# Two decoder layers on one core: five raw weight buffers instead of four, two half-tiles fewer, and one constant loaded later

## The chip, the cores and the metric

The kernel runs on one core of a Trainium2 chip. The time is the device time of one execution in microseconds (us), and the median of several runs is what counts. Besides the plain runs there is one profiled execution, from which the profile and the trace come. TensorE is called PE in them, its weight loads PEld, VectorE DVE, ScalarE ACT, GpSimd POOL and SyncE SP. SP only issues DMAs here.

## The reference

Two layers, each with three residual sub-layers on x of 512 tokens by 1024 features, all float32:

```
x += 1/2 * post(SwiGLU_1(pre(x)))          # 1024 -> 2 x 2816 -> 1024
h = pre(x);  P = h @ W_in                  # one projection for both branches
A = HGRN2 gated recurrence (4 heads)       # -> W_bA
B = sliding-window attention with sinks    # -> W_bB
x += post((sigmoid(gA)*A + sigmoid(gB)*B) @ W_out)
x += 1/2 * post(SwiGLU_2(pre(x)))

def swiglu(h, w_gate, w_up, w_down):
    return (jax.nn.silu(h @ w_gate) * (h @ w_up)) @ w_down
```

pre and post are RMS norms with gains of their own. The two SwiGLU networks of each layer, four in all, hold most of the arithmetic.

## The kernel before

**Products.** Every matrix product is done in three matmuls on operands split in two: a high part, which is the value cast to PE's reduced 32-bit type (fp32r), and a low part, the value minus its high part. `mm3` issues high x high, high x low, low x high. So each operand, weight or activation, needs a cast (on ACT) and a subtraction (on DVE) before PE can use it. For activations this is the function `split(src)`: line 400 casts on ACT, line 401 subtracts on DVE. For the weights it is the class `Stream` (object `ws`): `load` brings a raw unit of 128 x 1024 numbers from DRAM to a buffer "w" (lines 241 and 244, DMAs on SP's queue); `split` makes a pair `whi`, `wlo` out of it (cast at L324 on ACT; L331 subtracts on DVE, or, for some kinds of units, L328 and an accumulating DMA on POOL's queue, L329). There are `W32` raw buffers and `WS` = 6 pairs of `whi` and `wlo`. `ahead` splits as long as pairs are free: the pair of a unit comes free with the last matmul that reads it.

**An FFN.** After the first blocks, the function `fast` runs over blocks j of 128 hidden features. `sevenths` makes a block of gate and up with seven products in place of eight (a Strassen-like scheme, with sums of weights made in `split`, and sums of activations held in half-tiles); its copy of the first product is at L864 on ACT, its combinations on DVE are at L874, L876, L881 and L882. Then come Silu (L894, ACT) and the product with it (DVE), and the block z joins the list a. In the last block, `early` is called after the second of the seven products: it splits the first four blocks of a (`EARLY` = 4, with L400 and L401), so that the down product can begin at once:

```
def early():
    if j == FT - 1:
        for i in range(EARLY):
            a[i] = split(a[i])
```

The down product follows, in quarters and with seven products again. Its weights are quarter units: the function `quarter` sums raw units where needed (L267, L268, L276, L277, DVE), casts in two halves (L281, ACT, two casts a unit) and subtracts in two halves (L286, DVE). The raw units of a quarter come in four pieces, one DMA each. The sums need further quarters of the weight too, which `load` brings as a "side load" into eight half-tiles (L252, each in two pieces of 256 columns), issued right behind the load of a unit u that stands in `self.side`.

**Pools.** The half-tiles are all of one pool, tag "s", made by `big()`: 128 x 512 numbers, 2 KB a partition, `SLOTS` of them. The blocks of a, their splits, x's operands and their splits, the copies and sums of `sevenths` and of the down product and the side loads all take their slots there. A slot is given out in the order of the calls, and the new owner waits for the last reader of the old one.

**Order.** Only PE's order is written by hand: the tile framework is told that PE is scheduled manually, and an `Order` object interleaves generators by due times. The order on ACT, DVE and on the queues of SP and POOL is decided when the kernel is built, by the framework's scheduler, which sees when slots of the pools come free. SP's queue runs in order.

**Start.** The tiles of x (`xs[k]`, eight of them) are loaded in turn with the first `W32` raw units (`ws.load(k + 1)` where k < W32). Then the constants: `ident`, `half_ident` (the identity folded to 128 x 64, used in the mixer at L1015 to L1017), `dist`, `mask`, `lb_in`, `hgh` and `sink`.

Of the kernel before, what the change touches and what calls it, by code (L numbers as in the profile page):

```python
# [15 lines left out]
P = 128  # L16
# [10 lines left out]
EPS = 1e-6  # L27
LEVELS = (1, 2, 4, 8, 16, 32, 64)
MASKS = [(m, n) for b in LEVELS[:-1:2] for m, n in ((b, b), (2 * b, 2 * b), (2 * b, b))] + [(64, 64)]
SLOTS = 61  # L30

WAIT = dict(
    first=0.0, spread=2300.0, squares=1700.0, lay=34500.0, laid=770.0, normed=7600.0, final=2600.0,
    head=2600.0, level=1720.0, chunks=1270.0, blocks=350.0, norm=2370.0, gate=8000.0,
    values=1200.0, scores=2000.0, exp=9000.0, shares=4500.0, turn=1900.0, turned=3000.0, rest=1200.0, lent=3500.0, apart=4000.0, block=2000.0, pair=4000.0, att0=1260.0, att1=12300.0,
)
W32, WS, AHEAD, TAIL, PLAIN, FIRST, EARLY, LATE = 4, 6, 3, 4, 4, 7, 4, 8
TURN = 0
LEAD = 8
ORDER = ("p1", "p6", "p2", "p7", "p5", "p4", "p3")  # L40
# [5 lines left out]
def trunk(ctx: ExitStack, tc: tile.TileContext, xin, wall, gains, lbT, hgain, sinks, c_dist, c_mask, c_ident, out):  # L46
    nc = tc.nc
# [11 lines left out]
    def nm(s):  # L59
        seq[0] += 1  # L60
        return f"{s}_{seq[0]}"

    def big(dt=F32, shape=None):
        return sb.tile(shape or [P, S], dt, tag="s", name=nm("s"), bufs=SLOTS)

# [9 lines left out]
    def const(shape, name, dt=F32):  # L75
        return cp.tile(shape, dt, tag=name, name=name)
# [1216 lines left out]
            ws.load(k + 1)  # L1293
    ident = const([P, P], "ident")
    nc.sync.dma_start(ident, c_ident)
    half_ident = const([P, 64], "half_ident")
    nc.sync.dma_start(half_ident[:64], c_ident[:64, :64])
    nc.sync.dma_start(half_ident[64:], c_ident[64:, 64:])
    dist = const([P, 256], "dist")
    nc.sync.dma_start(dist, c_dist)  # L1300
    mask = const([P, len(MASKS) - 1, 32], "mask", I32)
# [5 lines left out]
    nc.sync.dma_start(hgh, hgain.partition_broadcast(P))  # L1307
    sink = const([P, DEPTH, NH], "sink")
    nc.sync.dma_start(sink, sinks.partition_broadcast(P))
    for k in range(KT):  # L1310
        pre.add(k)
        if k in (0, 2, 4):
            ws.split()
        if k > 2:
            pre.square(k - 3)
# [127 lines left out]
```

## Time and profile before

| what | before |
|---|---|
| median of 3 runs | 2112.13 us (2110.0 to 2112.33) |
| profiled execution | 2114.98 us |
| its span | 2113.2 us |
| mean granted clock of TensorE | 0.998 |

The span is the time from the first to the last instruction that the trace shows; the execution is somewhat longer. In the rows of a timeline stand the start and the duration in us, the engine, the line of the kernel, the operation and the tiles (`out<-in`), then partitions x elements; `x2` at the end means two such instructions in a row, shown in one line, and a bracket gives the idle time of the engine ahead of it with what ended it. In a row of waits stand the total time, how many times, and the longest. A row of groups gives the number of instructions, their busy time and the mean ns of one, then the idle time ahead of them and what ended it. A matmul's duration overlaps with the next one's: what counts is the distance between starts, 0.24 us for 512 columns at full clock.

### The profile page before, as it was taken

Reading aid. Unit: us, or ns where it says so; the run is one execution under the profiler, and the core shown is the slowest. Engines: PE = TensorE matmul, PEld = TensorE weight load, DVE = VectorE, ACT = ScalarE, POOL = GpSimd, SP = SyncE. Lnnn points to the kernel's source line nnn. Section 1 sums busy time; section 2 is a strip of 40 time slices with the busy share of each in tenths; the row PEclk is TensorE's granted clock in tenths of the full one; section 3 lists DMA queues with packets and bytes.
Section 4 is the critical chain, followed back from the end, with each engine's and each line's share of the span. In section 5 each row is a group of like instructions: output and inputs, shape, how many; then the busy total and the mean of one; then the engine's idle time right before and its main releaser. Section 6 shows DMA issues by size and latency. Waiting matters only on the chain.

```text
span 2113.2 us, 35244 instructions
## 1 busy us (share of the span) xinstructions
PE 2101.1 (99%) x13549; PEld 1875.3 (89%) x13549; DVE 1551.0 (73%) x2705; ACT 1124.9 (53%) x1900; POOL 154.6 (7%) x188
## 2 busy tenths in 40 slices
PE   9999999999999999999999999999999999999998
PEld 7899988887888999998899998888778989999987
DVE  5777886767676777779587778767686767777884
ACT  6555554446445555556355556454554545555562
POOL 0111000000000011110001110000000000111000
PEclk9999999999999999999999999999999999999999
DMA  7577754321237357774437775632122553677651
GB/s 234 150 181 181 188 146 137 106 70 61 70 100 209 120 125 175 180 194 125 160 109 175 181 185 150 189 116 95 51 71 70 135 185 110 154 182 181 183 165 45
DMA packets 148072, 298.36 MB, mean 141 GB/s; under 512 B 16992, under 2 KB 74816, under 8 KB 147904
## 3 DMA queue, kind: packets, MB, share of 16 engines
q1 hardware_dynamic: 122416, 228.16, 32.8%
q0 software_dynamic: 25344, 67.91, 18.5%
q8 instruction: 106, 1.74, 0.3%
q14 instruction: 62, 0.51, 0.1%
q10 hardware_dynamic: 144, 0.05, 0.0%
HBM read 213.43 MB, written 14.73 MB: 108 GB/s over the span
## 4 chain that ended last, share of the span: by engine, by line
PE 81%; DVE 9%; ACT 5%; issue 2%; DMA 2%; SPq 1%; ACTq 0%; DVEq 0%
PE acc L115 60%; PE aux L115 19%; ACT whi L324 2%; DMA w<-wall 2%; PE aux L125 1%; DVE s L401 1%; DVE wlo L331 1%; DVE wlo L286 1%; PE acc L125 1%; ACT s L400 1%; ACT m L894 1%; ACT wlo L328 1%; SPq L241 1%; DVE tt L268 0%; DVE w L267 0%
## 5 line engine op out<-in xcount | busy, mean ns | idle before, releaser
L115 PE MATMUL acc<-s,whi 128*128 128x256 f32 (+1 forms) x4968 | 1069.9, 312 | 1.7 <-ACT whi L324 0.9
L115 PEld LDWEIGHTS acc<-s,whi 128*128 128x128 f32 x4968 | 809.9, 191 | 54.5 <-issue 2.1
L115 PE MATMUL acc<-s,wlo 128*128 128x256 f32 (+1 forms) x2484 | 770.5, 310 | 0.1
L115 PEld LDWEIGHTS acc<-s,wlo 128*128 128x128 f32 x2484 | 474.5, 191 | 25.9 <-DVE wlo L331 0.4
L324 ACT CAST whi<-w 128x1024 fp32r<-128x1024 f32 (+1 forms) x341 | 317.4, 949 | 252.2 <-PE aux L115 103.4
L115 PE MATMUL acc<-whi,s 128*128 128x512 f32 x1264 | 413.6, 393 | 0.0
L324 ACT CAST whi<-tt 128x1024 fp32r<-128x1024 f32 x154 | 161.7, 1050 | 341.4 <-DVE tt L318 188.9
L331 DVE TENSOR_TENSOR wlo<-w,whi 128x1024 fp32r<-128x1024 f32 (+1 forms) x181 | 218.5, 1216 | 134.8 <-ACT whi L324 128.4
L115 PEld LDWEIGHTS acc<-whi,s 128*128 128x128 f32 x1264 | 237.0, 188 | 55.7 <-issue 3.2
L331 DVE TENSOR_TENSOR wlo<-tt,whi 128x1024 fp32r<-128x1024 f32 x154 | 188.2, 1222 | 102.5 <-ACT whi L324 102.5
L115 PE MATMUL acc<-wlo,s 128*128 128x512 f32 x632 | 246.8, 391 | 1.0 <-DVE wlo L286 1.0
L329 POOL DMA_DIRECT2D wlo<-w x160 | 138.2, 865 | 1266.3 <-ACT wlo L328 856.7
L115 PE MATMUL aux<-s,whi 128*128 128x256 f32 x1232 | 225.1, 283 | 0.0
L115 PE MATMUL aux<-whi,s 128*128 128x512 f32 x592 | 196.8, 390 | 0.0
L115 PEld LDWEIGHTS aux<-s,whi 128*128 128x128 f32 x1232 | 192.2, 192 | 0.0
L115 PE MATMUL aux<-s,wlo 128*128 128x256 f32 x616 | 174.4, 283 | 0.1
L115 PEld LDWEIGHTS acc<-wlo,s 128*128 128x128 f32 x632 | 118.7, 188 | 25.8 <-DVE wlo L286 2.4
L115 PEld LDWEIGHTS aux<-whi,s 128*128 128x128 f32 x592 | 111.1, 188 | 22.9
L328 ACT ACTIVATE wlo<-w 128x1024 fp32r<-128x1024 f32 (+1 forms) x160 | 129.9, 845 | 0.0
L400 ACT CAST s<-s 128x512 fp32r<-128x512 f32 (+1 forms) x164 | 88.6, 581 | 65.9 <-DVE s L459 60.6
L115 PEld LDWEIGHTS aux<-s,wlo 128*128 128x128 f32 x616 | 118.3, 192 | 0.3 <-DMA wlo<-w 0.3
L115 PE MATMUL aux<-wlo,s 128*128 128x512 f32 x296 | 115.2, 389 | 0.0
(185 smaller groups left out, 2136.6 us busy)
## 6 DMA issues: line engine op xcount, KB each, us to landing
w<-wall SPq DMA_DIRECT2D x267, 512.0 KB, 3.7
wlo<-w POOLq DMA_DIRECT2D x83, 512.0 KB, 5.5
w<-wall SPq DMA_DIRECT2D x288, 128.0 KB, 3.1
wlo<-w POOLq DMA_DIRECT2D x77, 256.0 KB, 3.3
x_d<-s SPq DMA_DIRECT2D x48, 256.0 KB, 2.1
s<-x_d SPq DMA_DIRECT2D x48, 256.0 KB, 5.5
w<-wall SPq DMA_DIRECT2D x34, 256.0 KB, 2.9
s<-wall SPq DMA_DIRECT2D x64, 128.0 KB, 3.5
```

Source lines behind the costliest of these rows:

```text
L115: nc.tensor.matmul(o, lhsT, rhs, start=start, stop=stop)
L125: nc.tensor.transpose(o, src, ident)
L241: nc.sync.dma_start(w.rearrange("p (m c) -> p m c", m=4) if c is None else w[:, c], a)
L286: nc.vector.tensor_tensor(it.lo[:, h[c]], w[c], it.hi[:, h[c]].bitcast(F32), op=ALU.subtract)
L324: i = nc.scalar.copy(it.hi[:, c], w[:, c])
L328: nc.scalar.mul(it.lo[:, c], w[:, c], -1.0)
L329: nc.gpsimd.dma_start(it.lo[:, c].bitcast(F32), w[:, c], accum_op=ALU.add)
L331: nc.vector.tensor_tensor(it.lo[:, c], w[:, c], it.hi[:, c].bitcast(F32), op=ALU.subtract)
L400: nc.scalar.copy(hi, src)
L401: nc.vector.tensor_tensor(lo, src, hi.bitcast(F32), op=ALU.subtract)
L894: nc.scalar.activation(out=m[:, 0:2, :], in_=m[:, 0:2, :], func=AF.Silu)
```

## The change

One raw weight buffer more (`W32`, 4 to 5, each of 4 KB a partition), two half-tiles fewer (`SLOTS`, 61 to 59, each of 2 KB a partition), and the two DMAs of `half_ident` issued after the other constants. At the start `W32` also sets how many raw units are loaded in turn with x's tiles, and in `Stream.split` and `quarter` how far the loads run ahead (`self.load(self.freed + W32)`).

```diff
-SLOTS = 61
+SLOTS = 59
...
-W32, WS, AHEAD, TAIL, PLAIN, FIRST, EARLY, LATE = 4, 6, 3, 4, 4, 7, 4, 8
+W32, WS, AHEAD, TAIL, PLAIN, FIRST, EARLY, LATE = 5, 6, 3, 4, 4, 7, 4, 8
...
     ident = const([P, P], "ident")
     nc.sync.dma_start(ident, c_ident)
-    half_ident = const([P, 64], "half_ident")
-    nc.sync.dma_start(half_ident[:64], c_ident[:64, :64])
-    nc.sync.dma_start(half_ident[64:], c_ident[64:, 64:])
     dist = const([P, 256], "dist")
...
     sink = const([P, DEPTH, NH], "sink")
     nc.sync.dma_start(sink, sinks.partition_broadcast(P))
+    half_ident = const([P, 64], "half_ident")
+    nc.sync.dma_start(half_ident[:64], c_ident[:64, :64])
+    nc.sync.dma_start(half_ident[64:], c_ident[64:, 64:])
     for k in range(KT):
         pre.add(k)
```

## The prediction

> **What bounds the kernel now.** I read the busy times first, then the shares of the chain that ended last, then what PE waited for.
>
> ```profile
> span 2113.2 us, 35244 instructions
> PE 2101.1 (99%) x13549; PEld 1875.3 (89%) x13549; DVE 1551.0 (73%) x2705; ACT 1124.9 (53%) x1900; POOL 154.6 (7%) x188
> PE 81%; DVE 9%; ACT 5%; issue 2%; DMA 2%; SPq 1%; ACTq 0%; DVEq 0%
> PE acc L115 <- DVE wlo L286: 1.0, 4, 0.3
> ```
>
> PE is busy for 2101.1 of 2113.2 us, so beside the clock nothing that the change does can win more than some 12 us, and an engine off the path matters only where it makes PE wait. The wait of PE that comes back is on the split of a quarter weight (L286), once in each of four FFNs. So I look at the places where buffers decide who goes first. The place that turns out to matter is where the fast loop of an FFN ends and the down product begins. Here are PE, ACT and DVE at the first of the four (the others end near 943, 1288 and 1986 us):
>
> ```profile
> 245.08 0.28 PE L115 MATMUL aux<-s,wlo 128*128 128x256 f32 x1
> 245.20 0.40 PE L115 MATMUL acc<-whi,s 128*128 128x512 f32 x1
> 245.44 0.40 PE L115 MATMUL acc<-wlo,s 128*128 128x512 f32 x1
> 245.67 0.62 PE L115 MATMUL acc<-whi,s 128*128 128x512 f32 x2
> ...
> 238.44 0.35 ACT L864 COPY s<-acc 128x256 f32<-128x256 f32 x1
> 238.69 0.62 ACT L400 CAST s<-s 128x512 fp32r<-128x512 f32 x1
> 239.21 1.05 ACT L324 CAST whi<-w 128x1024 fp32r<-128x1024 f32 x1
> 240.16 1.14 ACT L400 CAST s<-s 128x512 fp32r<-128x512 f32 x2
> 243.58 1.05 ACT L324 CAST whi<-w 128x1024 fp32r<-128x1024 f32 x1 [2.28 <-DMA w<-wall]
> 244.54 0.61 ACT L400 CAST s<-s 128x512 fp32r<-128x512 f32 x1
> 245.18 0.63 ACT L281 CAST whi<-w 128x512 fp32r<-128x512 f32 x1
> 246.33 0.63 ACT L281 CAST whi<-w 128x512 fp32r<-128x512 f32 x1 [0.52 <-DMA w<-wall]
> 247.83 0.63 ACT L281 CAST whi<-w 128x512 fp32r<-128x512 f32 x1 [0.87 <-DMA w<-wall]
> 248.74 0.63 ACT L281 CAST whi<-w 128x512 fp32r<-128x512 f32 x1 [0.29 <-DMA w<-wall]
> ...
> 246.41 0.69 DVE L874 TENSOR_TENSOR m<-acc,s 128x512 f32<-128x512 f32 x1
> 249.40 0.69 DVE L286 TENSOR_TENSOR wlo<-w,whi 128x512 fp32r<-128x512 f32 x1 [0.22 <-ACT whi L281]
> 250.01 0.68 DVE L876 TENSOR_TENSOR s<-acc,m 128x512 f32<-128x512 f32 x1
> ```
>
> The last matmul of the fast loop starts at 245.08, the first of the down product at 245.20, with no gap: its operand, the early split of a[0], was cast on ACT at 238.69. All four early casts (L400) and the L864 copy are over by 245.15, and only then come the four L281 casts of the first two quarter units, which wait for DMA pieces.
>
> **The change, part by part.** It takes two half-tiles of 2 KB a partition from pool "s", adds one raw buffer of 4 KB a partition, and moves half_ident's two DMAs on SP behind five other constants. The bytes are equal. No arithmetic is added or removed.
>
> The instruction orders of the two builds (not a view of the profile) tell more than the diff. PE's 13103 rows and POOL's stand in the same order. SP issues each raw load one place earlier: at the start the fifth raw load between xs[4] and xs[5], and at each FFN's end the first side load ahead of the first quarter unit's load. ACT and DVE change at four places only, the ends of the fast loops, apart from small swaps late in the down product that PE does not reach for microseconds. On ACT:
>
> ```
> before  L864, L400 a0, L324, L400 a1, L400 a2, L324, L400 a3, L281 x4, L894
> after   L324, L324, L281 x4, L864, L400 a0, L400 a1, L400 a2, L400 a3, L894
> ```
>
> The reason is the pool. The side load's eight half-tiles are now claimed earlier, out of 59 slots, and the early splits' slots come free only when the last block's operand tiles are released. DVE turns in the same way: L286 x4, L874, L401 x4, where L401 and L874 stood ahead of L286.
>
> (A) *PE's wait for a[0]'s high part.* The third and fourth L281 casts write a whi slot (six of them) that only the second-last matmul of the fast loop releases, so they can't start before about 245.1; and a[0]'s cast, which PE needs at 245.20, is now behind them. The raw data of the second unit should be no obstacle: its load now waits for the buffer that the first unit's load waits for today, so its pieces land when the first unit's do today, the last of them before 246.33, when today's second cast waits for it.
>
> ```profile
> L400 ACT CAST s<-s 128x512 fp32r<-128x512 f32 x136 | 79.2, 618 | 65.8 <-DVE s L459 60.6 <-DVE s L464 3.2 <-issue 2.0
> L401 DVE TENSOR_TENSOR s<-s,s 128x512 fp32r<-128x512 f32 x136 | 89.1, 687 | 13.1 <-ACT s L400 12.9
> L874 DVE TENSOR_TENSOR m<-acc,s 128x512 f32<-128x512 f32 x77 | 52.7, 685 | 11.4 <-PE acc L115 11.4
> L286 DVE TENSOR_TENSOR wlo<-w,whi 128x512 fp32r<-128x512 f32 x64 | 39.8, 686 | 0.7 <-ACT whi L281 0.7
> 1288.96 1.14 ACT L281 CAST whi<-w 128x512 fp32r<-128x512 f32 x2
> ```
>
> Two L281 casts in a row take 1.14 us, so they stand 0.52 apart; L864 to the next cast is 238.69 - 238.44 = 0.25. With the data in: 0.52 + 0.52 + 0.25 + 0.62 = 1.91, and some 0.1 until PE starts (my estimate), 2.0 us. If the fourth cast has to wait until 246.33: 1.13 + 0.52 + 0.25 + 0.62 + 0.1 = 2.6. I take 2.3 [2.0, 2.6].
>
> (B) *PE's second wait, for a[0]'s low part.* The third matmul needs it, 0.47 after the first (245.20 to 245.67). DVE must do the last L286 (0.60 apart, by the starts 249.40 and 250.01), L874, then L401 (0.687). With the casts as above the last L286 starts at 1.15 after the release, L874 at 1.75, L401 at 2.35, ending at 3.05; PE, started at 2.0, asks for it at 2.5 and waits about 0.6 to 0.7; with the later cast all of this shifts together. I take 0.7 [0.6, 0.75].
>
> What is queued behind: L400 of a[1] to a[3], 0.5 apart, and their L401, 0.60 apart, while PE uses each for three matmuls of 0.24; they keep up. L876 and L894 follow: with DVE's work only reordered, L876 ends within a microsecond of where it does now. Together 3.0 an FFN, four times: +12.0 [10.4, 13.4].
>
> (C) *The wait at product 7.* This is the wait on L286 above. DVE works almost without pause there and PE catches it up:
>
> ```profile
> 286.35 0.51 PE L115 MATMUL acc<-whi,s 128*128 128x512 f32 x1
> 287.14 0.50 PE L115 MATMUL acc<-wlo,s 128*128 128x512 f32 x1 [0.28 <-DVE wlo L286]
> ...
> 245.00:290.00 45.00, 44.72 (x197) 36.27 (x196) 41.52 (x76) 28.06 (x54) 3.45 (x4) 1.00 0.46 121
> ```
>
> (Columns of the stretch: length, then busy time of PE, PEld, DVE, ACT, POOL, then clock, DMA share, GB/s.) The two matmuls start 0.79 apart where 0.24 is usual: 0.55 lost. If PE comes 3 us later and DVE less than one, the loss goes: -0.5 each, -2.0 [-2.0, 0]. The row's own total, 1.0, lies inside.
>
> (D) *The clock.* PE would stand still for 3.0 of about 3.5 us. The trace shows what such holes do:
>
> ```profile
> 31.28:34.70 3.42, 2.33 (x15) 1.77 (x14) 1.62 (x3) 3.40 (x4) 1.41 (x2) 1.00 0.90 241
> 34.70:38.11 3.41, 3.41 (x10) 2.65 (x9) 0.87 (x2) 0.85 (x2) 0.46 (x1) 0.50 1.05 239
> 38.11:41.52 3.41, 2.70 (x10) 1.61 (x9) 1.29 (x2) 2.12 (x3) 0.00 (x0) 1.00 0.90 208
> 2103.17:2106.59 3.42, 1.03 (x5) 0.53 (x3) 1.89 (x4) 1.30 (x4) 0.00 (x0) 1.00 0.50 153
> 2106.59:2110.00 3.41, 1.97 (x8) 1.56 (x8) 1.77 (x3) 0.59 (x1) 0.00 (x0) 0.50 0.04 11
> ```
>
> After a stretch of 3.41 us with PE busy 2.33 or 1.03, the clock is 0.50 in the next; after 2.70 busy nothing of that is seen. At half clock a busy stretch loses half of 3.41, 1.7 us. Where both waits fall in one stretch PE is busy about 0.4 to 0.9; cut in two by a boundary, up to 1.9 in each. I expect it at three places of four: 3 x 1.7 = +5.1 [0, 6.8].
>
> The Trainium skill's page "TensorE: Matmul & The Clock Gate", section "HAM oscillation — how this bites in real kernels", gives the rule as no PE idle gaps above about 3.4 us. By it gaps of 2.3 and 0.7 would cost no clock, and the sum would be without the 5.1. The trace speaks against it: the hole at 33 us was 1.1 us long in one piece.
>
> (E) *The start.* The same ring holds the first weights:
>
> ```profile
> 22.73 1.05 ACT L324 CAST whi<-w 128x1024 fp32r<-128x1024 f32 x1 [4.35 <-DMA w<-wall]
> 24.01 1.06 ACT L324 CAST whi<-w 128x1024 fp32r<-128x1024 f32 x1 [0.23 <-DMA w<-wall]
> 32.99 1.05 PE L115 MATMUL aux<-ones,s 128*128 128x1 f32 x8 [1.09 <-DVE s L431]
> ```
>
> ACT stands 4.35 us for a weight load there, and PE 1.09 at 32.99. The fifth unit comes in earlier, but x's own tiles xs[5] to xs[7], which feed that wait, come one load later, and the two loads above are 1.28 apart. I take -0.5, with ±1.3 from that spacing.
>
> (F) *half_ident* costs nothing: 5.0 us from issue to landing, first used at 397.4 us.
>
> ```profile
> half_ident<-c_ident SPq DMA_DIRECT2D x2, 16.0 KB, 5.0
> L1015 DVE TENSOR_TENSOR s<-aux,half_ident x8: 416/418/425, 397.4 to 1580.8; 128x256 f32<-128x256 f32 x8
> ```
>
> What covers it is the whole first FFN, some 380 us; without that cover it would be those 5.0 us.
>
> *Sum:* +12.0 - 2.0 + 5.1 - 0.5 = +14.6. The profiled execution took 2114.98 us, 1.8 around its span and 2.85 above the median of 2112.13. So 2129.6 for a profiled execution like it, 2126.7 for the median.
>
> **The rivals.**
>
> *The waits, but the clock stays.* For it: at 38 us 0.7 us of idling in a stretch cost nothing, and of the 2.33 busy us before the throttled stretch about 1.05 were one-column matmuls (the eight at 32.99, in the start's rows), so I don't know where the limit lies. Against: 1.03 busy did throttle. 12.0 - 2.0 - 0.5 = +9.5, so 2121.6.
>
> *Worse: the second unit's pieces land as late as today.* If SP's order or the DMA rings, rather than the buffer, decide when they land, the fourth L281 cast stays at 248.74 and a[0]'s cast ends 248.74 + 0.52 + 0.25 + 0.62 = 250.1, 2.4 us later than in the worst of (A). For it: today these two casts do wait for their pieces. Against: the buffer that they wait for comes one release earlier. 14.6 + 4 x 2.4 = +24, 2136.
>
> *The other side, not slower.* The four L281 casts run earlier than I think: were their whi slots free and data in by about 242.4, 2.7 us before the release, a[0] would be cast in time, and the early loads would win what they can at (C) and (E): -2.0 - 1.3 = -3.3, 2108.8. The point from which it decides is the slot of the second unit: six of them, the sixth held to the last matmul but one. For it: ACT stands idle for 2.28 us before 243.58, so there is time. Against: the order of PE's reads is fixed and is the same.
>
> *The change does not do what it says* (no load sooner) is the worse case or, with ACT's order kept, no change; the build's order excludes the latter.
>
> **How the numbers follow.** Forecast 0.58, clock stays 0.20, worse 0.10, not slower 0.12. The likeliest gives 2126.7; its own range, from the ends above, is 2119 to 2133. Leaving out the worse and the not-slower case, 2118 to 2133. A measurement of this kernel tells 0.2%, 4.2 us, from no change: 2108.8 is within it, but of the not-slower case's 0.12 I give 0.04 to more than that (start and product 7 both better than bounded). So faster 0.04, same 0.08, slower 0.88.
>
> **What would show it.** (A) and (B): at each FFN's end PE waits on ACT s L400 for about 2.3 and on DVE s L401 for about 0.7, four times each, with L281 x4 ahead of L864 on ACT. (C): the row of PE on DVE wlo L286 gone. (D): clock 0.50 for a 3.41 us stretch behind three of the four. (E): the wait at 32.99 no longer than 1.1. The prediction is wrong if PE runs from the fast loop into the down product without a gap, or if L400 of a[0] stands ahead of L281 in the trace.

## The result, and the profile after

The changed kernel takes 2125.53 us (median of 4 runs, 2123.2 to 2129.26) beside 2112.23 us before (4 runs, 2110.0 to 2113.18): 1.0066 times as long, with a 95% interval of 1.0049 to 1.0084. It is slower, by some 13 us. The forecast was 2126.7. The profiled execution took 2129.26 us, its span was 2127.4.

First the busy times from the page of the changed kernel, then what PE waited for in it (total us, times, longest):

```profile
PE 2107.7 (99%) x13549; PEld 1880.7 (88%) x13549; DVE 1552.8 (73%) x2705; ACT 1124.2 (53%) x1900; POOL 154.2 (7%) x188
```

```profile
PE acc L115 <- ACT s L400: 8.1, 4, 2.3
PE acc L125 <- DVE s L730: 2.9, 1, 2.9
PE aux L115 <- DVE s L431: 1.4, 1, 1.4
...
PE acc L115 <- DVE s L401: 0.9, 3, 0.5
```

DVE, ACT and POOL are busy as long as before within 2 us: no work was added. PE is busy 6.6 us longer with the same 13549 matmuls, so a part of the loss is not waiting but slower matmuls. A row that did not exist before heads the list of waits: L400, four times, 8.1 us. The row of L286 is gone.

Now the first of the four places, the end of the first FFN's fast loop, in the timelines of PE, ACT and DVE (start, us, engine, what):

```profile
244.53 0.28 PE L115 MATMUL aux<-s,wlo 128*128 128x256 f32 x1
247.11 0.80 PE L115 MATMUL acc<-whi,s 128*128 128x512 f32 x1 [2.31 <-ACT s L400]
247.71 0.63 PE L115 MATMUL acc<-wlo,s 128*128 128x512 f32 x1
248.25 1.22 PE L115 MATMUL acc<-whi,s 128*128 128x512 f32 x2
...
243.33 1.14 ACT L281 CAST whi<-w 128x512 fp32r<-128x512 f32 x2 [1.83 <-PE aux L115]
244.73 0.62 ACT L281 CAST whi<-w 128x512 fp32r<-128x512 f32 x1 [0.25 <-PE aux L115]
245.65 0.62 ACT L281 CAST whi<-w 128x512 fp32r<-128x512 f32 x1 [0.31 <-DMA w<-wall]
246.18 0.37 ACT L864 COPY s<-acc 128x256 f32<-128x256 f32 x1
246.44 2.18 ACT L400 CAST s<-s 128x512 fp32r<-128x512 f32 x4
...
246.30 0.69 DVE L286 TENSOR_TENSOR wlo<-w,whi 128x512 fp32r<-128x512 f32 x1 [0.23 <-ACT whi L281]
246.91 0.69 DVE L874 TENSOR_TENSOR m<-acc,s 128x512 f32<-128x512 f32 x1
247.51 2.49 DVE L401 TENSOR_TENSOR s<-s,s 128x512 fp32r<-128x512 f32 x4
```

The third L281 cast is held by PE, that is by a whi slot that PE still reads, and starts 0.20 us after the start of the fast loop's last matmul; the fourth waits 0.31 for its piece; L864 and the casts of a[0] to a[3], which PE needs at once, stand behind. The first matmul of the down product starts 2.58 us after the last one of the loop, where 0.12 was between them before.

And the clock, in stretches of 3.41 us whose ends are the times at which it changes (length, busy time of PE, PEld, DVE, ACT, POOL, granted clock, DMA share, GB/s), at the first, second and fourth place:

```profile
243.28:246.70 3.42, 1.53 (x13) 1.32 (x12) 2.38 (x4) 2.81 (x6) 0.00 (x0) 1.00 0.81 220
246.70:250.11 3.41, 3.00 (x6) 1.99 (x7) 3.41 (x7) 1.92 (x4) 0.00 (x0) 0.50 0.93 298
250.11:253.52 3.41, 3.41 (x9) 2.63 (x8) 2.62 (x6) 0.92 (x2) 0.00 (x0) 0.50 0.79 255
946.43:949.84 3.41, 1.46 (x11) 1.22 (x10) 3.00 (x5) 3.16 (x7) 0.00 (x0) 1.00 0.79 222
949.84:953.26 3.42, 3.20 (x8) 2.10 (x7) 3.39 (x7) 1.17 (x3) 0.00 (x0) 0.50 0.90 290
...
1997.74:2001.15 3.41, 1.80 (x7) 1.18 (x8) 3.41 (x6) 2.63 (x6) 0.00 (x0) 1.00 0.82 238
2001.15:2004.56 3.41, 3.41 (x10) 2.63 (x9) 2.62 (x6) 0.92 (x2) 0.00 (x0) 0.50 0.80 241
```

Behind each hole the next stretch runs at 0.50, and two of them behind the first.

PE's order is the same in both kernels, so the starts of the same matmul can be subtracted, after minus before; this difference is called the drift. Its account for the two profiled executions, in us:

| where | drift | step |
|---|---|---|
| start, at the 161st matmul (40.75 us before) | -0.22 | |
| before the first FFN's end | -0.56 | -0.56 |
| after it / product 7 | +4.98 / +4.17 | +5.54 / -0.81 |
| before and after the second | +4.13, +8.14 / +7.33 | +4.01 / -0.81 |
| before and after the third | +7.15, +11.09 / +10.28 | +3.94 / -0.81 |
| before and after the fourth | +10.24, +14.79 / +14.32 | +4.55 / -0.47 |
| last matmul | +14.27 | |

The steps are 18.04 at the four FFN ends and -2.90 at the four product 7 waits; what is left is the -0.56 ahead of the first FFN's end and 0.3 of small drifts. Product 7 runs on without a gap (it lost 0.55 there before, between the starts at 286.35 and 287.14):

```profile
290.97 0.61 PE L115 MATMUL acc<-whi,s 128*128 128x512 f32 x2
291.42 0.39 PE L115 MATMUL acc<-wlo,s 128*128 128x512 f32 x1
```

### The profile page after: what moved, and what is told of

The parts are those of the page before. It is cut to its first block, busy times and chain, and to the rows that moved or that the text cites. A ratio compares the mean times of both kernels' runs of the same rounds, so it can differ in the third digit from the quotient of the medians.

```text
span 2127.4 us, 35256 instructions
## 1 busy us (share of the span) xinstructions
PE 2107.7 (99%) x13549; PEld 1880.7 (88%) x13549; DVE 1552.8 (73%) x2705; ACT 1124.2 (53%) x1900; POOL 154.2 (7%) x188
## 4 chain that ended last, share of the span: by engine, by line
PE 88%; DVE 0%; DMA 0%; ACT 0%; issue 0%; SPq 0%; DVEq 0%
PE acc L115 64%; PE aux L115 22%; PE aux L125 1%; PE acc L125 1%; DMA wlo<-w 0%; DMA w<-wall 0%; ACT whi L281 0%; DVE wlo L286 0%; DVE s L401 0%; DVE m L874 0%; SPq L241 0%; DVE s L730 0%; ACT s L599 0%; DVE s L711 0%; ACT s L722 0%
## 5 line engine op out<-in xcount | busy, mean ns | idle before, releaser
L115 PE MATMUL acc<-whi,s 128*128 128x512 f32 x1264 | 418.6, 398 | 8.9 <-ACT s L400 8.1
L400 ACT CAST s<-s 128x512 fp32r<-128x512 f32 (+1 forms) x164 | 87.6, 580 | 66.8 <-DVE s L459 61.4
```

What stands on the lines that cost most here:

```text
L115: nc.tensor.matmul(o, lhsT, rhs, start=start, stop=stop)
L400: nc.scalar.copy(hi, src)
```

## The experiments

Each run was compared with the kernel before on the same chip; the medians of before were 2114.78 us beside the first four, 2113.31 beside the next four, 2112.76 beside the last two. So the ratios count.

**1. Four raw buffers again** (the half-tiles stay at 59, half_ident stays late).

```diff
-W32, WS, AHEAD, TAIL, PLAIN, FIRST, EARLY, LATE = 5, 6, 3, 4, 4, 7, 4, 8
+W32, WS, AHEAD, TAIL, PLAIN, FIRST, EARLY, LATE = 4, 6, 3, 4, 4, 7, 4, 8
```

> The changed kernel with four raw buffers again; 59 half-tiles and the late half_ident stay. Theory (the fifth buffer, by moving the side load ahead, turns ACT's and DVE's order at the FFNs' ends; the half-tiles and half_ident cost nothing): ACT's order as before, no wait of PE on L400, 2112 us (2109.5 to 2114.5). Rival (the pool's two slots are what makes the early splits late): the waits on L400 stay, 2120 to 2126 us. Rival (half_ident's place costs at the start): the drift stands at the first 50 us, 2114 to 2118 us.

Measured: 2111.99 us, ratio 0.999 [0.9981, 1.0]. No wait on L400 at the FFNs' ends; the wait on L286 is there, 1.2 us in four. The drift against the kernel before stays within 0.6 us from the first matmul to the last, in the start too. With four buffers, the two half-tiles and half_ident's place are worth nothing that shows; the loss comes with the fifth buffer.

**2. The side load one unit later** (five buffers, 59 half-tiles).

```diff
-                self.side[u + 1] = [pieces(j0 + q, 1) for q in range(4)]
+                self.side[u + 2] = [pieces(j0 + q, 1) for q in range(4)]
```

> The changed kernel, five buffers and all, with the side load issued one unit later. Theory (what counts is where the side load stands against the quarter units, not the fifth buffer as such): L864 and L400 ahead of the L281 casts again, no wait of PE on L400, no half clock at the FFNs' ends, the wait on L286 at product 7 back (four times 0.3 us in the waits), 2111.5 us (2109 to 2114). Rival (raw loads one place earlier crowd the early splits by themselves): waits on L400 stay, above 2118 us.

Measured: 2108.28 us, ratio 0.9974 [0.9963, 0.9986]: faster than both kernels. ACT at the first FFN's end, and what PE still waits for:

```profile
234.78 0.36 ACT L864 COPY s<-acc 128x256 f32<-128x256 f32 x1
235.03 0.62 ACT L400 CAST s<-s 128x512 fp32r<-128x512 f32 x1
235.55 1.06 ACT L324 CAST whi<-w 128x1024 fp32r<-128x1024 f32 x1
236.50 1.15 ACT L400 CAST s<-s 128x512 fp32r<-128x512 f32 x2
237.54 1.06 ACT L324 CAST whi<-w 128x1024 fp32r<-128x1024 f32 x1
238.49 0.63 ACT L400 CAST s<-s 128x512 fp32r<-128x512 f32 x1
240.04 1.14 ACT L281 CAST whi<-w 128x512 fp32r<-128x512 f32 x2 [0.92 <-ACT s L400]
241.43 0.62 ACT L281 CAST whi<-w 128x512 fp32r<-128x512 f32 x1 [0.25 <-PE aux L115]
```

```profile
PE acc L125 <- DVE s L730: 2.8, 1, 2.8
PE aux L115 <- DVE eps_t L138: 1.1, 1, 1.1
PE acc L115 <- DVE s L904: 0.7, 1, 0.7
```

The order is that of the kernel before, and the waits on L400 and L401 are gone with it. The fifth buffer as such is not the cost. Two things came otherwise than expected. The product 7 wait did not come back (it wins 0.81, 0.81, 0.81 and 0.48 in the drift): the quarter units' data now come one load earlier, so the casts at 240.04 and 241.43 wait for no DMA, where the kernel before lost 0.52, 0.87 and 0.29 there, and PE finds the split of product 7 done. And the start won 3.5 us: the wait on L431 is gone, and so is the half clock behind it.

**3. The side load one unit earlier in the kernel before** (four buffers).

```diff
-                self.side[u + 1] = [pieces(j0 + q, 1) for q in range(4)]
+                self.side[u + 0] = [pieces(j0 + q, 1) for q in range(4)]
```

> The kernel before, four buffers, with the side load issued one unit earlier. Theory (the side load's place alone does it): two L281 casts stand ahead of L864 and the four L400; at the first FFN a[0]'s cast comes after the first unit's last piece, 1.13 + 0.52 + 0.25 + 0.62 + 0.1 = 2.6 us of waiting, about 2.0 to 2.5 at the others, half clock for one stretch behind each (1.7), the product 7 wait gone: 4 x (2.3 + 0.2 + 1.7 - 0.6) = +14, 2126 us (2120 to 2129). Rival (it takes the whi slot that the second unit waits for, so the fifth buffer): waits on L400 below 1 us each, no half clock, 2111 to 2115 us.

Measured: 2132.47 us, ratio 1.0084 [1.0069, 1.0099], worse than the change itself. PE's waits and ACT at the first place:

```profile
PE acc L115 <- ACT s L400: 11.9, 6, 3.5
...
PE acc L115 <- DVE s L401: 1.4, 3, 0.6
...
PE acc L115 <- DVE wlo L286: 0.9, 3, 0.3
```

```profile
245.22 0.62 ACT L281 CAST whi<-w 128x512 fp32r<-128x512 f32 x1 [0.16 <-DMA w<-wall]
246.45 0.62 ACT L281 CAST whi<-w 128x512 fp32r<-128x512 f32 x1 [0.61 <-DMA w<-wall]
246.97 0.37 ACT L864 COPY s<-acc 128x256 f32<-128x256 f32 x1
247.24 2.18 ACT L400 CAST s<-s 128x512 fp32r<-128x512 f32 x4
```

With two casts ahead in place of four, and held by data in place of a slot, the loss is there, with all 61 half-tiles: the place of the side load among the loads is what turns ACT's order. It came out a little above the range that was expected. The expected gain at product 7 did not come: each place had put PE off by 4.5 to 5.4 us in the drift, but the wait on L286 stayed in three of four. Nor did the half clock come at each place, only at the third and fourth. At the first, PE stood still for 2.50 us, longer than at any FFN's end of the changed kernel, and at the second for 2.33, each across the end of a stretch, and full clock followed (stretches as above, at the first place):

```profile
243.60:247.01 3.41, 1.81 (x16) 1.61 (x14) 1.83 (x2) 2.23 (x4) 0.00 (x0) 1.00 0.80 228
247.01:250.43 3.42, 2.12 (x8) 1.46 (x9) 3.33 (x6) 2.40 (x6) 0.00 (x0) 1.00 0.90 272
250.43:253.84 3.41, 3.41 (x17) 2.82 (x16) 1.99 (x4) 0.00 (x0) 0.00 (x0) 1.00 0.85 243
```

At these two places PE waited for an L400 cast once more, 1.1 us at the first and 0.65 at the second, some 14 us behind the loop's end, so that their drift comes near to that of the other two.

**4. PE kept busy in the hole** (the changed kernel; the extra matmuls go into a tile that the down product starts afresh).

```diff
             late = Late(src, LEAD)
+            for _ in range(5):
+                nc.tensor.matmul(y[0][0][:, :256], ident, dist, start=True, stop=True)
```

> The changed kernel with five extra matmuls (identity by 256 columns, float32) ahead of each down product, about 2.1 us, into a PSUM tile that the product then starts afresh; they only fill PE's wait. Theory (half of the loss is the clock, which falls because PE stands still): no stretch at 0.50 behind the FFNs' ends, PE's wait on L400 nearly gone from the list but the product starting no earlier than in the changed kernel, the wait on L401 back at 0.6 each: 2125.5 - 8.4 + 4 x 0.4 + 4 x 0.2 = 2119.5 us (2117 to 2122). Rival (the half clock has another cause, or gaps of 2.3 us don't cause it): stretches at 0.50 as in the changed kernel, 2125 to 2128 us.

Measured: 2121.23 us, ratio 1.003 [1.0019, 1.0042]. PE at the first place, where x10 are the five extra matmuls, two records each:

```profile
242.49 0.28 PE L115 MATMUL aux<-s,wlo 128*128 128x256 f32 x1
242.61 2.32 PE L683 MATMUL acc<-dist,ident 128*128 128x256 f32 x10
245.69 0.50 PE L115 MATMUL acc<-whi,s 128*128 128x512 f32 x1 [0.77 <-ACT s L400]
...
246.83 0.73 PE L115 MATMUL acc<-whi,s 128*128 128x512 f32 x2 [0.40 <-DVE s L401]
```

No stretch of the trace behind an FFN's end is below full clock, and the four places cost 3.68, 3.08, 3.28 and 2.96 us, 13.0 in all, against 18.04 in the profile of the changed kernel (and 15.9 in its second profile, experiment 9), though the product starts no earlier after the last matmul of the loop: 3.20 us here, 2.58 there. So the half clock was 3 to 5 us of the loss, and it came from PE's standing still.

**5. The early casts held ahead** (the changed kernel, side load as in the change; instructions marked with `pin` keep the program's order on their engine).

```diff
-            nc.scalar.copy(hi, src)
+            i = nc.scalar.copy(hi, src)
+            if early[0]:
+                pin(i)
...
-                nc.scalar.copy(it.hi[:, h[c]], w[c])
+                pin(nc.scalar.copy(it.hi[:, h[c]], w[c]))
```

(`early[0]` is true while the first four blocks are split in the last block of the fast loop.)

> The changed kernel, five buffers and early side load as they are, but the early splits' casts (L400 of a[0] to a[3]) and the quarter units' casts (L281) are held in the order in which the program names them, so that a[0]'s cast stands ahead of the L281 casts on ACT. Theory (the loss is ACT's order at the FFNs' ends alone): PE's waits on L400 and L401 gone, no half clock there, 3 to 6 us below the kernel before on the same chip, as the run with the side load one unit later. Rival (the early side load takes the slots that the early splits need, so they are late in any order): PE still waits 1 to 2.5 us on L400 four times, 4 to 12 us above the kernel before.

Measured: 2108.07 us, ratio 0.9973 [0.9963, 0.9983]. ACT at the first place (L868, L402, L900 are L864, L400, L894; the loop's last matmul starts at 242.13):

```profile
239.02 0.36 ACT L868 COPY s<-acc 128x256 f32<-128x256 f32 x1
239.28 2.18 ACT L402 CAST s<-s 128x512 fp32r<-128x512 f32 x4
245.13 0.63 ACT L900 ACTIVATE m<-m 128x512 f32<-128x512 f32 x1 [3.67 <-DVE m L886]
```

The first early cast starts 2.85 us ahead of the loop's last matmul and the fourth is over 0.67 ahead of it, with the side load as early as in the change. The L281 casts, which stood in front in the change, begin at 248.44 here, and PE waits for none of them. So the slots of the early casts were free in time: the loss lies in the order in which ACT was given its instructions, not in the pool.

**6 and 8. Where the gain of experiment 2 comes from**: four units instead of five loaded in turn with x's tiles (in experiment 2's kernel), and experiment 2 once more.

```diff
-        if k < W32:
+        if k < 4:
             ws.load(k + 1)
```

> The changed kernel with the side load one unit later, and four raw units instead of five loaded in turn with x's tiles at the start. Theory (the gain of that run has two parts, 2.4 us at the four product 7 waits through earlier quarter loads, and up to 3.5 us at the start through the fifth unit between x's tiles): the wait on L431 near 33 us and the half clock behind it are back, product 7 stays without a wait, 2.4 us below the kernel before. Rival (the start differs between executions, whatever is loaded): start as in that run, 5 to 6 us below the kernel before.

> The run with five buffers and the side load one unit later once more, beside the others on one chip. Theory: 0.2 to 0.35% below the kernel before, with no wait on L431 above 0.5 us at the start. Rival (the start's part was luck of that execution): 0.1 to 0.2% below, and the wait on L431 at about 1 us.

Measured: 2108.44 us, ratio 0.9982 [0.9972, 0.9991], and 2108.19 us, ratio 0.9976 [0.9966, 0.9985]. The two drifts are alike: -3.11 and -3.09 at the 161st matmul, about -2.9 at the four product 7 waits together, no wait on L431 in either. So the start's gain does not need the fifth load between x's tiles: it was expected to go, and stayed in this profile, where SP issues the fifth load behind the constants, at 16.56 us. But four of the ten executions of experiment 6 took 2109.87 to 2111.26, and none of the nine of experiment 8 more than 2108.73, so the load may still count for how often the gain is had.

**7. PE late, but never idle** (the kernel before, with seven extra matmuls as in experiment 4).

> The kernel before with seven extra matmuls (identity by 256 columns, float32), 0.43 us each, 3.0 us in all, ahead of each down product, so that PE comes 3 us later and never stands still. Theory of the prediction (C): PE's lateness by itself removes the product 7 wait, 4 x 3.0 - 2.4 = 9.6 us above the kernel before, no half clock at the FFNs' ends, no row of PE on DVE wlo L286. Rival (DVE follows PE, and only earlier loads remove the wait): the row stays at about 1 us in four, 12 us above.

Measured: 2121.86 us, ratio 1.004 [1.0025, 1.0055], some 8.5 us. At the first place:

```profile
244.20 3.18 PE L683 MATMUL acc<-dist,ident 128*128 128x256 f32 x14
247.04 0.58 PE L115 MATMUL acc<-whi,s 128*128 128x512 f32 x1
```

The four delays show in the drift as 2.84, 2.92, 2.90 and 3.03; no clock is lost there; the row of L286 is gone from PE's waits, and product 7 gives back 0.81 three times and 0.48. The sum is 11.69 - 2.91 = 8.8. PE's lateness alone is enough to remove that wait, if DVE's order is left as it is.

This profile shows something at the start too. It has four buffers, and PE waits 1.1 us for L431 as in the kernel before, but no half clock follows (the stretch with that wait, and the next):

```profile
32.90:36.31 3.41, 2.43 (x15) 2.17 (x16) 0.89 (x2) 3.38 (x5) 1.86 (x2) 1.00 0.84 250
36.31:39.72 3.41, 3.05 (x12) 1.84 (x10) 1.27 (x3) 1.15 (x3) 0.00 (x0) 1.00 1.08 232
```

The drift falls by 1.6 there, to -0.68 at the 161st matmul. So that half clock can stay away without the fifth buffer.

**9. The changed kernel again, and 10. half_ident back in its place** (in experiment 2's kernel).

> The changed kernel once more, on one chip with the next run. Its first profile showed 0.2 us won at the start and a wait of 1.4 us on L431, where four others with five buffers won 2.6 to 3.9 us there. Theory (same loads at the start, so that execution merely had late data): drift of 1.5 to 3.5 us below the kernel before at 40 us, waits on L400 at the four FFN ends of 1.9 to 2.6 each as before, 0.45 to 0.7% above the kernel before. Rival (the early side load or its order takes the start's gain away): drift at 40 us below 0.5 us again.

> Five buffers, the side load one unit later, and half_ident's two DMAs back in their old place, right behind ident. Theory (the constant's place is worth nothing: it lands hundreds of us before its use, and 16 KB cost the queue next to nothing): the same as the run with the side load one unit later, 0.2 to 0.3% below the kernel before, start won as there. Rival (the two small DMAs hold up the weight loads behind them at the start): the start's gain is smaller by 0.5 to 1.5 us or gone, with the half clock near 35 us back.

Measured: 2124.89 us, ratio 1.0059 [1.0044, 1.0074]; and 2108.06 us, ratio 0.9976 [0.9966, 0.9986], with the start as in experiment 2. In the second profile of the changed kernel the drift is -2.42 at the 161st matmul, where the first had -0.22, and the half clock near 35 us is missing: how much the start wins differs between executions of the same kernel. Its four steps at the FFN ends are 3.96, 4.43, 4.40 and 3.11. At the fourth, PE stood still as long, but across a boundary:

```profile
1992.41:1995.83 3.42, 1.65 (x14) 1.44 (x13) 2.41 (x4) 2.83 (x6) 0.00 (x0) 1.00 0.76 230
1995.83:1999.24 3.41, 2.62 (x10) 1.88 (x11) 3.41 (x7) 1.89 (x4) 0.00 (x0) 1.00 0.81 239
```

No stretch below full clock follows, and the place costs 3.11 in place of 4.4.

## Why the prediction was right, step by step

**(A) The wait for a[0]'s high part: right.** 8.1 us in four waits, the longest 2.3, where 4 x 2.3 = 9.2 was taken and 2.0 each was the lower bound. The chain was the predicted one: L281 held by a whi slot, L864, L400.

**Its reason: in part right.** The prediction put the turned order down to the side load's earlier claim on a pool of 59 slots, and to early splits that get their slots only at the end. The side load's earlier place is shown to be the cause: moved back, it heals the change (experiment 2), moved ahead, it harms the kernel before (3). A lack of slots is not: 59 slots with four buffers cost nothing (1), the order turns with 61 as well (3), and the first early cast can start 2.85 us ahead of the loop's end with the very same pool (5). Why the build's scheduler places the casts behind when the side load is early stays open, and whether its count of free slots has a part in that; that was not tried.

**(B) The wait for a[0]'s low part: the row is there, but small.** 0.9 us in three waits, where 2.8 was taken. The size failed mostly because of (D): at half clock PE takes 0.54 to 0.60 a matmul (247.11, 247.71, 248.25), so it asks for the low part 1.1 us after the first matmul, not 0.47, and DVE has caught up. Where the clock stayed, the wait was there four times, but still shorter than 0.7: 1.7 in all, 0.5 at the longest (experiment 4).

**(D) The clock: right in kind, and the terms (B) and (D) belong together.** All four places were throttled in the first profile, three in the second; three of four was forecast. By place, the cost was 3.1 with no stretch at half clock, 3.9 to 4.6 with one, 5.5 with two. So one stretch costs 0.8 to 1.4 net (3.94 and 4.55 less 3.11), less than the 1.7 of a fully busy stretch; part of the difference is the wait for DVE, which a slow PE hardly has. The executions of the changed kernel fit: the one with a mean clock of 0.998 took 2123.2 us, the one with 0.994 took 2129.26. (A), (B) and (D) together were forecast as 12.0 + 5.1 = 17.1 and measured as 18.04 and 15.9 (3.96 + 4.43 + 4.40 + 3.11) in the two profiles. By the Trainium skill's rule (the page "TensorE: Matmul & The Clock Gate", section "HAM oscillation — how this bites in real kernels"), no PE idle gaps above about 3.4 us, these holes would have cost no clock. The traces differ: in the two profiles of the changed kernel, holes of 1.9 to 2.3 us were followed by half clock seven times in eight, and experiment 4 shows the hole to be the cause. But the prediction's sign for it, how long PE is busy in a stretch, does not decide alone: 1.80 was followed by half clock here, and 1.81 was not in experiment 3. So it is in part luck that three of four came so near.

**(C) Product 7: right in place and sign, a little larger.** -2.90 for -2.0. The reason given, PE's lateness, is enough by itself (7). But the fifth buffer alone does the same through earlier data (2), which the prediction had not seen, and lateness was not enough in (3), where DVE's order was turned too and the wait stayed in three of four.

**(E) The start: taken too small.** -0.5 was taken, with 1.3 to either side. At the 161st matmul the first profile shows -0.22, the second -2.42, and the other five-buffer runs (2, 4, 5, 6, 8 and 10) between -2.25 and -3.53; the four-buffer runs (1, 3 and 7) show 0.38, 0.27 and -0.68. So seven of the eight five-buffer profiles lie beyond the better end, -1.8. (The drift falls by another 0.2 to 0.35 near 241 us, but in the four-buffer runs too, so that is not the change's.) The term left out is the clock: in all the five-buffer runs but the first profile the half clock behind the wait on L431 is missing. Not all of that is the buffer's, since one of the four profiles with four buffers goes without it too (7).

**(F) half_ident: right**, nothing with four buffers (1) and nothing with five (10).

**The sum: near in part by luck.** The terms that were missed have both signs. In the first profile the FFN ends cost 0.9 more than forecast and product 7 gave back 0.9 more. In the second the FFN ends cost 1.2 less and the start won more, and the last matmul came 9.48 us later than before, where 14.6 was forecast. Both are subtracted from one execution of the kernel before, which itself was 2.85 above its median.

The rivals: *the clock stays* happened at one place of eight; *the other side* is shown to be a matter of ACT's order alone, since with the order of before the same five buffers win 5 us (2, 5), more than the 3.3 given there (which took -1.3 for (E), whose better end was -1.8); *worse*, the second unit's pieces as late as today, did not come, though in the first FFN the fourth cast waited 0.31 for one.

## What to carry to other kernels

A buffer added to a ring moves every load that is issued at a count of released buffers, and also what is hung on those loads, as the side loads were here. Look in the build's order for what crossed what on each engine, above all a late-blocked instruction that came to stand ahead of one that the bounding engine needs next: here four casts of 0.62 us cost 13 us, and pinning the order, or moving the side load by one unit, turns the same buffer into a gain of 5 us. When a hole opens in front of the busiest engine, price its clock too, and together with the wait behind it, since each shrinks the other.

## What the runs showed of the hardware that was not expected

The same hole can throttle the clock or not. The stretches at half clock of one trace begin whole multiples of 3.413 us apart (246.70 - 35.07 = 211.63 = 62.0 x 3.413; 949.84 - 246.70 = 206.0 x 3.413), so a hole can lie inside one stretch of this grid or across the end of one. A stretch with PE busy 1.53, 1.46 or 1.80 of 3.41 was followed by half clock; one with 1.65 followed by one with 2.62 was not (9), and neither was one with 1.81 followed by one with 2.12 (3). The busy time alone doesn't draw the line: 2.33 at 31.28 us, partly one-column matmuls, throttled, and 2.12 in experiment 3 did not. What does draw it, no run here tells. In the first FFN one hole cost two stretches, 246.70 to 253.52, although PE was busy for 3.00 of the first; why, no run tells either.
